# Forming the second 256 features' share of four heads' values one round earlier, beside the modulation

## The chip, the cores and the metric

The kernel runs on one core of one Trainium2 chip. The core has a matrix engine (TensorE, "PE" in the rows, with its weight loads as "PEld"), a vector engine (VectorE, "DVE"), a scalar engine (ScalarE, "ACT"), GpSimd ("POOL") and SyncE ("SP"), which here does nothing but issue transfers. Matrix results go to PSUM, which this kernel uses as eight banks of 128x512 float32. The metric is the time of one execution on the device, in microseconds (us); lower is better.

## The reference

One layer of a diffusion backbone: 256 latent tokens `x` and 256 context tokens `ctx`, each with 2048 features. What matters here is its beginning:

```python
mod = jax.nn.silu(c) @ w_mod[l] + b_mod[l]          # six vectors of 2048
sh_m, sc_m, ga_m, sh_f, sc_f, ga_f = split(mod)
hc = modulate(rms_norm(ctx, g), shc_m, scc_m)       # context, from silu(c_ctx)
h  = modulate(rms_norm(x, g), sh_m, sc_m)           # modulate(h, shift, scale) = h*(1+scale) + shift
p_i, p_ff, p_fb, p_q, p_g, p_cv, p_cg, p_gc, p_gh = split_proj(h @ w_in[l])
# context: only the first three parts of hc @ w_in
o = hgrn_bidir(q_prep(p_q), to_heads(p_i), hgrn_forget(p_ff), hgrn_forget(p_fb), ...)
```

So before any projection can be formed, the shift and the scale of a feature must be known, for the latent and for the context tokens. `p_i` are the values of 8 heads of 128 columns, for both kinds of tokens. A gated recurrence over the heads, a convolution branch, a gated merge, an output projection and a squared-ReLU MLP follow.

## The kernel before, in words

Every matrix product is formed in three terms: both factors are split into a high part and the rest (`hi`, `lo`), and hi*hi, hi*lo and lo*hi are added up in PSUM. A weight tile is 128x1024 float32 (512 KB). SyncE loads it into one of five `raw` buffers, ScalarE writes its `whi` (L123), VectorE its `wlo` (L126); each of these has four buffers. The class `Stream` holds the order of all loads as a list, `fetch_to` keeps up to 13 loads ahead, and a load into `raw` waits until the buffer's last reader is through. The order of the instructions on each engine is fixed when the program is built.

The front of the kernel computes the shift and the scale and uses them as soon as they are there. It is a loop over eight rounds `c = 0..7`, one for each 256 features. A round loads two `wmd` tiles (last 512 rows of the modulation weights, transposed), six `wm` tiles (its first 1536 rows, into `rawpage`), one `wi0` tile (256 rows of the input projection, columns of the first four heads' values) and in rounds 0, 1, 3 and 5 one `wf0` tile (forget gates of head 0). In a round

- VectorE forms eight sums of products with the `wmd` tiles (L648, four a tile),
- TensorE multiplies the `wm` tiles (`bank<-rawpage,s`, the modulation matmuls; the trace counts them as 24), ScalarE copies the sum (L605), TensorE turns it, VectorE makes scale and shift of it (L612 to L619),
- ScalarE and VectorE form the modulated features `h` (L629, L632), and VectorE multiplies the next round's inputs `xT` with their norm (L555),
- TensorE forms the values of the first four heads for these features (`values(0, ...)`, 24 matmuls a round in a steady order, half a round late) and the forget gates of head 0 (12 matmuls a round, `forget`).

The modulation matmuls stand at the end of a round's work: round c's other matmuls, then the modulation matmuls of round c + 1. In the rows below a round is counted from the end of its modulation matmuls.

The four accumulators of `values(0)` and the two of `forget` keep six of the eight banks through the front. One more product is formed there: the values of the *second* four heads over the *first* 256 features, from the tile `wi0[8]`, at the end of round 0 (`values_begun`): 24 matmuls, in two pairs of banks for the two kinds of tokens, copied to the pages `v1` by ScalarE. After the front, `values(1, ...)` forms the second four heads' values over the other seven tiles (`wi0[9]` to `wi0[15]`), and adds `v1` on VectorE at the end (L1322). This stretch is called the tail here. In it VectorE also begins the dot products of the other modulation vectors (L1244, tiles `wmt`), which need a row of silu(c) (`silu_row`, loaded at L1254 behind the front). The blocks of q and the heads follow.

`self.queued = []` ahead of the front makes TensorE keep the program's order there.

Of the kernel before, what the change touches and what calls it, by code (L numbers as in the profile page):

```python
# [8 lines left out]
F32 = mybir.dt.float32  # L9
# [4 lines left out]
ALU = mybir.AluOpType  # L14
# [4 lines left out]
KT = D // P  # L19
# [17 lines left out]
RAWS = 5  # L37
KP = 12
FETCH = 13

# [96 lines left out]
class Kernel:  # L137
# [227 lines left out]
    def run(self):  # L365
        nc, a = self.nc, self.a
# [3 lines left out]
        v = self.v  # L370
# [46 lines left out]
        for c in range(8):  # L417
            for u in range(2):
                st.add_whole(a["wmd"][2 * c + u])
            for t in range(KP // 2):  # L420
                st.add_whole(a["wm0"][KP // 2 * c + t], paged=True)
            st.add(a["wi0"][c])
            if c == 0 or c % 2 and c < 7:
                st.add(a["wf0"][(c + 1) // 2])
            if c == 0:
                st.add(a["wi0"][8])
        gq = collections.deque()
# [8 lines left out]
        def gemv(n):  # L436
            for _ in range(n):
                if gq:
                    st.add_gemv(*gq.popleft())
# [4 lines left out]

        for j in range(9, 16):
            st.add(a["wi0"][j])
            gemv(2)
        for b in range(16, 24):
# [215 lines left out]
        for c in range(8):  # L664
# [35 lines left out]
            if c % 2 and c < 7:  # L700
                parts(fq, *self.last2)
            if c < 7:
                normed(c + 1, *self.last2)
            for _ in range(2 if c else 1):
                next(values)
            for _ in range(2):
                next(forget)
            if c == 0:
                vb = self.values_begun(hx, vq2.popleft())
        for _ in values:  # L710
# [580 lines left out]
    def values(self, ch, hx, tiles, begun=None):  # L1291
# [3 lines left out]
        accs = [self.bank() for _ in range(4)]  # L1295
        for kq in range(begun is not None, 8):
            hi, lo = tiles()
            for k2 in range(2):
                k = 2 * kq + k2
                s = slice(k2 * 512, (k2 + 1) * 512)  # L1300
                cuts = [(accs[2 * i + tb], slice(tb * P, (tb + 1) * P), *hx(i)(k)[:2]) for i in range(2) for tb in range(2)]
                first, last = k == 2 * (begun is not None), k == KT - 1

# [22 lines left out]

    def values_begun(self, hx, w):

        nc = self.nc
        pages = self.pages(2, F32, "v1")  # L1330
        for i in range(2):
            accs = [self.bank() for _ in range(2)]
            for k in range(2):
                s = slice(k * 512, (k + 1) * 512)
                xh, xl = hx(i)(k)[:2]
                for tb in range(2):
# [4 lines left out]
            for tb in range(2):  # L1341
                self.last4 = nc.scalar.copy(out=pages[i][:, tb * 512:(tb + 1) * 512], in_=accs[tb])
        return pages
# [275 lines left out]
```

## Time and profile before

| | |
|---|---|
| median of 3 runs | 1643.31 us (1642.83 to 1644.01) |
| the profiled execution's own time | 1643.43 us |
| its span, first to last instruction | 1641.7 us |
| TensorE, matmuls busy | 1627.7 us (99%) |
| TensorE, weight loads busy | 1357.7 us (83%) |
| VectorE / ScalarE busy | 1163.2 us (71%) / 799.7 us (49%) |
| read from HBM | 370.93 MB |

A matmul counts as busy from its start to a modelled end; matmuls overlap, so a busy share of 99% means that there is nearly always one under way, not that none could be added. The 1.7 us between the span and the execution's time lie around the instructions. Times in rows count from the first instruction.

### The profile page before, as it was taken

The numbers are of one execution on the slowest core, as the hardware profiler recorded it, in microseconds if no ns is written. First come the engines' busy times: TensorE is split into PE (matmuls) and PEld (weight loads), VectorE is DVE, ScalarE is ACT, GpSimd is POOL, SyncE is SP. The second block draws the span as 40 slices with busy tenths as digits, with TensorE's granted clock in tenths as the row PEclk, the third lists the DMA queues.
The fourth block names the chain that finished last, engine by engine and source line by source line (L and its number), as shares of the span: only waits on it lengthen the run. The fifth ranks groups of instructions, "written<-read, shape, count | busy, mean of one in ns | idle before, by whom it ended". The sixth has DMA issues, their size and how long they took to land.

```text
span 1641.7 us, 22004 instructions
## 1 busy us (share of the span) xinstructions
PE 1627.7 (99%) x8207; PEld 1357.7 (83%) x8207; DVE 1163.2 (71%) x1702; ACT 799.7 (49%) x1141; POOL 8.1 (0%) x18
## 2 busy tenths in 40 slices
PE   8999999999999999999999999999999999999998
PEld 6668888888988888888788888888888888888887
DVE  7777877777868889967887766456655665566555
ACT  6553444343554444653446665445544554346543
POOL 0000000000000000000000000000000000000000
PEclk9999999999999999999999999999999999999999
DMA  9998954444656566678887466677666666665553
GB/s 378 392 395 293 316 166 141 154 142 142 207 189 224 187 192 206 230 271 306 313 289 260 143 230 205 214 235 241 218 206 231 234 213 217 230 219 195 190 193 116
DMA packets 103484, 374.47 MB, mean 228 GB/s; under 512 B 11601, under 2 KB 11857, under 8 KB 103377
## 3 DMA queue, kind: packets, MB, share of 16 engines
q1 hardware_dynamic: 101952, 368.60, 65.8%
q0 software_dynamic: 1280, 4.21, 0.8%
q8 instruction: 64, 1.05, 0.3%
q14 instruction: 44, 0.35, 0.1%
q10 hardware_dynamic: 144, 0.26, 0.0%
HBM read 370.93 MB, written 2.10 MB: 227 GB/s over the span
## 4 chain that ended last, share of the span: by engine, by line
PE 94%; DVE 2%; DMA 2%; ACT 1%; issue 1%; SPq 0%; DVEq 0%; ACTq 0%
PE bank L185 62%; PE bank L252 18%; PE bank L254 9%; PE bank L1391 2%; DMA x<-ctx 1%; DVE wlo L126 1%; DMA rawpage<-wm 1%; PE bank L1422 0%; DMA raw<-wpw 0%; PE bank L1433 0%; PE bank L1431 0%; ACT whi L123 0%; ACT h L629 0%; SPq L498 0%; ACT xT L629 0%
## 5 line engine op out<-in xcount | busy, mean ns | idle before, releaser
L126 DVE TENSOR_TENSOR wlo<-raw,whi 128x1024 fp32r<-128x1024 f32 x488 | 594.0, 1223 | 356.2 <-ACT whi L123 348.0
L123 ACT ACTIVATE whi<-raw 128x1024 fp32r<-128x1024 f32 x488 | 513.5, 1059 | 576.9 <-PE bank L185 320.7
L185 PE MATMUL bank<-whi,h 128*128 128x512 f32 x1264 | 396.3, 391 | 0.8 <-ACT h L629 0.5
L252 PE MATMUL bank<-h,whi 128*128 128x512 f32 x1280 | 322.3, 394 | 0.0
L185 PEld LDWEIGHTS bank<-whi,h 128*128 128x128 f32 x1264 | 237.1, 188 | 51.0 <-DVE h L1080 0.7
L252 PEld LDWEIGHTS bank<-h,whi 128*128 128x128 f32 x1280 | 230.4, 189 | 41.6
L185 PE MATMUL bank<-wlo,h 128*128 128x512 f32 x632 | 246.5, 390 | 0.8 <-DVE wlo L126 0.8
L185 PE MATMUL bank<-whi,hidh 128*128 128x512 f32 x503 | 195.1, 388 | 0.0
L185 PE MATMUL bank<-wlo,hidh 128*128 128x512 f32 x503 | 195.1, 388 | 0.0
L185 PE MATMUL bank<-whi,hidl 128*128 128x512 f32 x503 | 195.0, 388 | 0.0
L254 PEld LDWEIGHTS bank<-h,wlo 128*128 128x128 f32 x1280 | 174.6, 190 | 12.6
L254 PE MATMUL bank<-h,wlo 128*128 128x256 f32 x1280 | 178.4, 282 | 0.0
L185 PE MATMUL bank<-h,whi 128*128 128x512 f32 x512 | 164.6, 402 | 0.0
L185 PEld LDWEIGHTS bank<-wlo,h 128*128 128x128 f32 x632 | 118.7, 188 | 26.6 <-DVE wlo L126 2.5
L185 PEld LDWEIGHTS bank<-whi,hidl 128*128 128x128 f32 x503 | 94.4, 188 | 19.5
L185 PEld LDWEIGHTS bank<-wlo,hidh 128*128 128x128 f32 x503 | 94.5, 188 | 19.3
L185 PEld LDWEIGHTS bank<-whi,hidh 128*128 128x128 f32 x503 | 94.5, 188 | 19.2
L185 PEld LDWEIGHTS bank<-h,whi 128*128 128x128 f32 x512 | 92.0, 189 | 21.5 <-issue 5.9
L185 PE MATMUL bank<-h,wlo 128*128 128x512 f32 x256 | 100.0, 391 | 0.0
L1244 DVE SCALAR_TENSOR_TENSOR raw<-raw,silu_row 128x1024 f32<-128x1024 f32 x64 | 76.6, 1218 | 0.2 <-DMA raw<-wmt 0.2
L1231 DVE SCALAR_TENSOR_TENSOR gacc<-raw,silu_c,gacc 128x1024 f32<-128x1024 f32 x60 | 76.6, 1277 | 0.0
L185 PEld LDWEIGHTS bank<-h,wlo 128*128 128x128 f32 x256 | 48.1, 188 | 10.6 <-DVE wlo L126 0.3
(246 smaller groups left out, 1359.8 us busy)
## 6 DMA issues: line engine op xcount, KB each, us to landing
raw<-w SPq DMA_DIRECT2D x256, 512.0 KB, 4.2
raw<-wi SPq DMA_DIRECT2D x172, 512.0 KB, 4.4
raw<-wmt SPq DMA_DIRECT2D x64, 512.0 KB, 4.2
raw<-wm SPq DMA_DIRECT2D x64, 512.0 KB, 4.5
rawpage<-wm SPq DMA_DIRECT2D x48, 512.0 KB, 8.6
raw<-wo SPq DMA_DIRECT2D x32, 512.0 KB, 4.8
raw<-wmd SPq DMA_DIRECT2D x16, 512.0 KB, 8.2
raw<-who SPq DMA_DIRECT2D x16, 512.0 KB, 4.9
```

Source lines behind the costliest of these rows:

```text
L123: kn.his.append(nc.scalar.activation(out=hi, in_=raw, func=AF.Copy))
L126: kn.los.append(nc.vector.tensor_tensor(lo, raw, hi.bitcast(F32), op=ALU.subtract))
L185: ins = fn(*args, **kw)
L252: nc.tensor.matmul(bank, w[0][:, cut(i)], x(k)[2], start=(k == 0), stop=False)
L254: nc.tensor.matmul(bank[:, T:], w[1][:, cut(i)], x(k)[0], start=False, stop=(k == nk - 1))
L1231: nc.vector.scalar_tensor_tensor(acc, raw, s, acc, op0=ALU.mult, op1=ALU.add)
L1244: nc.vector.scalar_tensor_tensor(raw, raw, 1.0, self.srow, op0=ALU.mult, op1=ALU.mult, accum_out=self.dot[:, 32 * j + b:32 * j + b + 1])
L1391: nc.tensor.matmul(ps[:, b * P:(b + 1) * P], w, r, start=True, stop=True)
```

## The change

A constant `BEGUN = 2` says how many tiles of the second four heads' values are formed in the front. The tile `wi0[9]` is loaded at the end of round 1's loads and split there; `values_begun` runs in rounds 0 and 1, and the second time adds its result to the pages `v1` on VectorE, in place of ScalarE's copy. `values(1)` begins with `wi0[10]`. The loads of `wmt` that stood behind `wi0[9]` are given to the next tiles.

```diff
@@ Kernel.run, the list of loads
             st.add(a["wi0"][c])
             if c == 0 or c % 2 and c < 7:
                 st.add(a["wf0"][(c + 1) // 2])
-            if c == 0:
-                st.add(a["wi0"][8])
+            if c < BEGUN:
+                st.add(a["wi0"][8 + c])
...
-        for j in range(9, 16):
+        for j in range(8 + BEGUN, 16):
             st.add(a["wi0"][j])
-            gemv(2)
+            gemv(2 + (j < 12))
@@ the front's loop
             if c % 2 and c < 7:
                 parts(fq, *self.last2)
+            if c and c < BEGUN:
+                parts(vq2, *self.last2)
             if c < 7:
                 normed(c + 1, *self.last2)
...
-            if c == 0:
-                vb = self.values_begun(hx, vq2.popleft())
+            if c < BEGUN:
+                vb = self.values_begun(hx, vq2.popleft(), c, c and vb)
@@ values
-        for kq in range(begun is not None, 8):
+        begins = BEGUN * (begun is not None)
+        for kq in range(begins, 8):
...
-                first, last = k == 2 * (begun is not None), k == KT - 1
+                first, last = k == 2 * begins, k == KT - 1
@@ values_begun
-    def values_begun(self, hx, w):
+    def values_begun(self, hx, w, c, pages):
...
-        pages = self.pages(2, F32, "v1")
+        pages = pages or self.pages(2, F32, "v1")
...
-                xh, xl = hx(i)(k)[:2]
+                xh, xl = hx(i)(2 * c + k)[:2]
...
-                self.last4 = nc.scalar.copy(out=pages[i][:, tb * 512:(tb + 1) * 512], in_=accs[tb])
+                v = pages[i][:, tb * 512:(tb + 1) * 512]
+                if c:
+                    nc.vector.tensor_tensor(v, accs[tb], v, op=ALU.add)
+                else:
+                    nc.scalar.copy(out=v, in_=accs[tb])
```

On TensorE, at the end of round 1 (`h2` and `h3` are the features of round 1, `whi_400` the forget tile), before:

```order
L185 MATMUL bank_431<-h2_545,wlo_401 128x512
L185 MATMUL bank_432<-h2_545,whi_400 128x512 x2
L185 MATMUL bank_432<-h2_545,wlo_401 128x512
L185 MATMUL bank_615<-rawpage_488,s32_82 32x512 [waits DMAHW0_49,PE_49]
L185 MATMUL bank_615<-rawpage_488,s32_82 32x512
```

The forget gates are followed by the modulation matmuls of round 2. With the change (`whi_561`, `wlo_562` are of the tile `wi0[9]`; names in brackets are semaphores that the instruction waits for):

```order
L186 MATMUL bank_432<-h2_545,wlo_401 128x512
L186 MATMUL bank_596<-whi_561,h2_545 128x512 [waits Activation_49]
L186 MATMUL bank_596<-wlo_562,h2_545 128x512 [waits DVE_49]
L186 MATMUL bank_596<-whi_561,h2_545 128x512
L186 MATMUL bank_597<-whi_561,h2_545 128x512 [waits PE_49]
...
L186 MATMUL bank_612<-whi_561,h2_545 128x512 [waits DVE_49]
L186 MATMUL bank_612<-wlo_562,h2_545 128x512
L186 MATMUL bank_612<-whi_561,h2_545 128x512
L186 MATMUL bank_613<-whi_561,h2_545 128x512 [waits DVE_49]
...
L186 MATMUL bank_653<-rawpage_499,s32_82 32x512 [waits DMAHW1_49,DVE_49]
```

Between them stand 24 matmuls of the new tile, in the bank pairs 596, 597 (latent tokens) and 612, 613 (context tokens); the first of each of the second pair waits for VectorE, and so does the first modulation matmul of round 2.

On VectorE, from round 1's `xT` to round 2's `cols`, before (`junk` and `raw` are the eight sums for round 2):

```order
L555 TENSOR_TENSOR xT_110<-xT_110,s_82 128x1024
L126 TENSOR_TENSOR wlo<-raw,whi 128x1024
L648 SCALAR_TENSOR_TENSOR junk,part<-raw,srow 128x512 x2
L648 SCALAR_TENSOR_TENSOR raw,part<-raw,srow 128x512 x2
L648 SCALAR_TENSOR_TENSOR junk,part<-raw,srow 128x512 x2
L648 SCALAR_TENSOR_TENSOR raw,part<-raw,srow 128x512 x2
L653 TENSOR_TENSOR part<-part,pack 128x4
L612 TENSOR_REDUCE cols<-bank 128x8
```

and with the change:

```order
L556 TENSOR_TENSOR xT_110<-xT_110,s_82 128x1024
L127 TENSOR_TENSOR wlo<-raw,whi 128x1024 x2
L649 SCALAR_TENSOR_TENSOR junk,part<-raw,srow 128x512 x2
L649 SCALAR_TENSOR_TENSOR raw,part<-raw,srow 128x512 x2
L1348 TENSOR_TENSOR v_439<-bank,v_439 128x512 x2
L649 SCALAR_TENSOR_TENSOR junk,part<-raw,srow 128x512 x2
L649 SCALAR_TENSOR_TENSOR raw,part<-raw,srow 128x512
L1348 TENSOR_TENSOR v_440<-bank,v_440 128x512 x2
L649 SCALAR_TENSOR_TENSOR raw,part<-raw,srow 128x512
L654 TENSOR_TENSOR part<-part,pack 128x4 x2
L613 TENSOR_REDUCE cols<-bank 128x8
```

A second `wlo` stands ahead of the sums, and the four adds to `v1` stand among them.

On SyncE one load of `wi` is added behind round 1's `wf`, and the one of `wi0[9]` behind the front is gone; the order of the others is unchanged but for the `wmt` loads.

## Rows read from the trace of the kernel before

**Rows 1.** The page: its span, the busy times of the engines, and the clock that was granted to TensorE in 40 equal slices of the span (9 is 90% or more).

```profile
span 1641.7 us, 22004 instructions
PE 1627.7 (99%) x8207; PEld 1357.7 (83%) x8207; DVE 1163.2 (71%) x1702; ACT 799.7 (49%) x1141; POOL 8.1 (0%) x18
PEclk9999999999999999999999999999999999999999
```

**Rows 2.** Busy times in windows: rounds 1 to 6 of the front, each from the end of its modulation matmuls to the end of the next round's, and the tail; between them lies round 7 with the end of the front. Columns: the window and its length, busy us of each engine (and instructions), granted clock, share of the DMA engines, GB/s.

```profile
43.63:55.20 11.57, 11.57 (x69) 7.67 (x65) 7.79 (x18) 6.54 (x11) 0.00 (x0) 1.00 1.01 395
55.20:66.79 11.59, 11.59 (x68) 7.67 (x65) 9.30 (x28) 5.60 (x10) 0.00 (x0) 1.00 1.02 410
66.79:80.08 13.29, 12.84 (x68) 7.71 (x64) 11.01 (x30) 6.55 (x11) 0.00 (x0) 1.00 0.97 370
80.08:92.05 11.97, 11.97 (x66) 7.79 (x65) 9.69 (x29) 5.59 (x10) 0.00 (x0) 1.00 1.02 409
92.05:104.67 12.62, 12.62 (x66) 7.79 (x64) 9.89 (x26) 6.54 (x11) 0.00 (x0) 1.00 1.03 409
104.67:116.22 11.55, 11.55 (x66) 7.73 (x64) 9.26 (x27) 5.60 (x10) 0.00 (x0) 1.00 1.03 409
129.07:167.15 38.08, 38.08 (x169) 31.53 (x168) 30.83 (x45) 11.35 (x13) 0.00 (x0) 1.00 0.86 307
```

**Rows 3.** The list of waits of TensorE's weight loads in rounds 1 to 7 (43.6 to 130): who waited for whom, us in total, times, the longest.

```profile
PEld bank L185 <- DMA rawpage<-wm: 4.4, 7, 1.1
```

**Rows 4.** The chain of work that ended last, in round 3 (60 to 82): start, length, what; and SyncE's own time line for the pairs of `wmd` loads of rounds 4 and 6 (start of the first issue, time to the end of the second).

```profile
65.41 1.23 DVE raw L648 x4
66.66 0.33 SPq L85
...
70.02 9.04 DMA rawpage<-wm
79.10 3.10 PE bank L185 x14
...
59.41 7.58 SPq L85 DMA_DIRECT2D raw<-wmd  x2
84.20 6.75 SPq L85 DMA_DIRECT2D raw<-wmd  x2
```

**Rows 5.** TensorE's time line at the end of round 1: the last forget matmuls and the modulation matmuls of round 2.

```profile
52.17 0.39 PE L185 MATMUL bank<-h,wlo 128*128 128x512 f32 x1
52.48 2.78 PE L185 MATMUL bank<-rawpage,s 128*32 128x512 f32 x24
```

**Rows 6.** VectorE's time line in rounds 1 and 2 (the first three rows of round 1, the last two are the first and the fourth sum for round 3), and ScalarE's in round 1.

```profile
50.41 1.22 DVE L555 TENSOR_TENSOR xT<-xT,s 128x1024 f32<-128x1024 f32 x1
51.54 1.22 DVE L126 TENSOR_TENSOR wlo<-raw,whi 128x1024 fp32r<-128x1024 f32 x1
52.68 0.69 DVE L648 SCALAR_TENSOR_TENSOR junk<-raw,srow 128x512 f32<-128x512 f32 x1
64.10 0.68 DVE L648 SCALAR_TENSOR_TENSOR junk<-raw,srow 128x512 f32<-128x512 f32 x1
65.94 0.68 DVE L648 SCALAR_TENSOR_TENSOR raw<-raw,srow 128x512 f32<-128x512 f32 x1
...
49.67 1.04 ACT L123 ACTIVATE whi<-raw 128x1024 fp32r<-128x1024 f32 x1
55.34 0.59 ACT L605 COPY row<-bank 128x512 f32<-128x512 f32 x1 [4.62 <-PE bank L185]
```

**Rows 7.** The add of a bank to `v1` on VectorE, at the end of the tail: shortest, median and longest ns.

```profile
L1322 DVE TENSOR_TENSOR v<-bank,v x4: 686/690/691, 165.3 to 168.4; 128x512 f32<-128x512 f32 x4
```

**Rows 8.** The loads of line L85 from 5 to 135 us: time from issue to landing.

```profile
DMA to landing us min/median/max: 3.1/9.0/10.9
```

**Rows 9.** The end of the front and the tail in the time lines of SyncE (the load of the tail's third tile, the load of the row of silu(c), the load of the tail's fourth tile), VectorE (third `wlo`, first and second dot product, fourth and fifth `wlo`) and ScalarE (third `whi`, the gates, the row's sigmoid, fourth `whi`).

```profile
125.12 0.33 SPq L85 DMA_DIRECT2D raw<-wi  x1
125.98 0.42 SPq L1254 DMA_DIRECT2D silu_row<-crow  x1
136.28 0.33 SPq L85 DMA_DIRECT2D raw<-wi  x1
...
129.63 1.23 DVE L126 TENSOR_TENSOR wlo<-raw,whi 128x1024 fp32r<-128x1024 f32 x1 [4.53 <-ACT whi L123]
133.87 1.23 DVE L1244 SCALAR_TENSOR_TENSOR raw<-raw,silu_row 128x1024 f32<-128x1024 f32 x1
135.03 1.22 DVE L1244 SCALAR_TENSOR_TENSOR raw<-raw,silu_row 128x1024 f32<-128x1024 f32 x1
142.01 1.23 DVE L126 TENSOR_TENSOR wlo<-raw,whi 128x1024 fp32r<-128x1024 f32 x1 [1.18 <-ACT whi L123]
146.74 1.23 DVE L126 TENSOR_TENSOR wlo<-raw,whi 128x1024 fp32r<-128x1024 f32 x1 [1.12 <-ACT whi L123]
...
128.53 1.06 ACT L123 ACTIVATE whi<-raw 128x1024 fp32r<-128x1024 f32 x1
130.91 1.09 ACT L598 ACTIVATE fg<-bank 128x512 f32<-128x512 f32 x2
131.88 1.15 ACT L1263 ACTIVATE sig<-silu_row 128x512 f32<-128x512 f32 x2
140.92 1.06 ACT L123 ACTIVATE whi<-raw 128x1024 fp32r<-128x1024 f32 x1 [7.89 <-DMA raw<-wi]
```

More of the change, by code (lines that the diff above doesn't have):

```diff
@@ L38 @@
 KP = 12
+BEGUN = 2
 FETCH = 13
```

## The prediction

> **What bounds the kernel now.** I read the page first. TensorE (PE) is busy 99% of the span at full granted clock [rows 1], so nothing far from PE can give much, and work that is only moved pays exactly where PE waits today. The windows, cut at the end of each round's modulation matmuls, show where that is: the rounds last 11.57, 11.59, 13.29, 11.97, 12.62 and 11.55 us [rows 2]. A round holds the same PE work each time, so 11.57 is PE's own need, and what lies above it (1.72 + 0.40 + 1.05, less 0.02 = 3.15 us) is waiting. The list of waits names whom: PE's weight loads for `rawpage<-wm`, 4.4 us in 7 waits [rows 3], a part of which lies beside running matmuls. The transfers move 409 GB/s at a share of 1.03 in an undisturbed round and only 370 at 0.97 in the round of 13.29 us [rows 2]: there the queue ran thin. The chain says why [rows 4]: VectorE (DVE) ended four sums at 66.64, this freed a `raw` buffer, SyncE issued at 66.66, and six loads later, at 79.06, PE went on. So the front has two bounds that lie close together, PE (11.57 a round) and the transfers, and the second hangs on DVE's sums through five buffers.
>
> **The change, part by part.**
>
> *Taken out and put in.* 24 matmuls leave the tail and enter the end of round 1, where in front of the 12 modulation matmuls PE had nothing between 52.17 and 52.48 [rows 5]. A tile of values is 24 matmuls; in the tail seven of them (168) take 38.08 us [rows 2], so one is 5.44 us, 0.2267 a matmul. Their price is the same in both places; this is no gain by itself.
>
> *Waits in round 1.* The new matmuls need the new tile's `wlo`. On DVE it stands behind `wlo` of the forget tile, which starts at 51.54 and is followed at 52.68 by the next instruction [rows 6]; so the new one runs 52.68 to 53.9 (1.22 each). PE can start its first new matmul at 52.40, the second only at 53.92: 1.3 us lost. All eight banks are in use then (4 values, 2 forget, 2 that alternate), so the two pairs of accumulators and the next modulation bank pass through two banks; each waits for an add on DVE. An add of this form takes 0.69 us [rows 7]. Pair 1 is complete with the ninth and the twelfth matmul, whose ends are 53.92 + 7 x 0.2267 + 0.39 = 55.9 and 56.6; DVE's first four sums last 2.52 us as in the next round (64.10 to 66.62) [rows 6], hence to 56.3, and the adds end at 57.0 and 57.6. Pair 2 starts at 57.0 instead of 56.4 (0.55 lost). Its adds stand behind three more sums (a quarter of 2.52 each), the first runs 59.4 to 60.1, and only then the modulation matmuls of round 2 start: 60.09 against 52.48. Sum: 5.44 + 1.3 + 0.55 + 0.3 = 7.6 us later. Round 2 begins at 62.8 instead of 55.20. ScalarE is no bound: the new tile's `whi` follows the one at 49.67, ahead of 4.6 us of idle time [rows 6].
>
> *What PE gets back.* With no wait at all PE would run 5 rounds of 11.57 from 62.8 and begin round 7 at 120.65; before it was 116.22 [rows 2]. So the front ends at least 4.4 us later: 7.6 less the 3.15 of waits.
>
> *What the loads do.* One load more in round 1 is 512 KB at 409 GB/s, 1.28 us. More important is the buffer ring. The second `wmd` load of round 4 takes the buffer of the first of round 3, so it waits for DVE's first four sums for round 3, which stand behind round 2's whole chain. In round 1 `xT` starts 6.78 us after the round's begin (43.63 to 50.41) and lasts 1.13, then 2.52 us of sums [rows 6]: with round 2 at 62.8 the load is issued at 73.3, not 66.66. Meanwhile the queue has little: the loads before it were issued long ago and are through at about 70 (69 plus the 1.28). Upper bound for the way from this issue to the last modulation load of round 4: what it takes now, 66.66 to 79.06, 12.4 us [rows 4]; lower bound: the shortest landing of this line, 3.1 us [rows 8], plus six transfers of 1.28, 10.8 us. This gives 84.1 to 85.7; I take 85.0, nearer the present case, since that one too restarted behind a thin queue. PE goes on 1.02 us after that landing (79.06 to 80.08), so round 4 begins at 86.0, just where PE alone would be (85.95). From there 28 transfers (nine a round and one forget tile) follow each other to the last modulation load of round 7: 28 x 1.28 = 35.8, so 120.8, and round 7 begins at 121.9. Delay at the front's end: 5.65 us, bounds 4.4 (PE alone) and 6.4 (85.7 instead of 85.0).
>
> The Trainium skill's page "DMA: Bandwidth & Descriptors", section "Anatomy of one DMA — SWDGE (gpsimd) path", gives a DMA a fixed 2.0 us plus its bytes at 436 GB/s, here an estimate of 3.2 us for the first load and 1.2 for each that follows: 83.7 instead of 85.0, and PE alone would then set the pace (the second rival). No row splits a transfer into these two parts; the shortest landing, 3.1 us [rows 8], lies near that estimate.
>
> *The tail.* Its values have 24 matmuls less: -5.44. But the third of its six tiles was not early. Before, its `wlo` ended at 143.24, and PE needed it at 129.07 + 3 x 5.44 + 0.23 = 145.62 [rows 2, 9]: 2.38 us ahead, as the fourth tile from the tail's begin. Now it is the third, needed 5.44 us sooner after the tail's begin. What it waits for is not PE: its load takes the buffer that the second dot product frees (136.25, issue 136.28), the dots wait for the row of silu(c), and that row's load is issued behind the last tile that the front's end prepares [rows 9]. All this starts from round 7 and moves with it. Only ScalarE has one `whi` less ahead of the gates, which may bring the row's sigmoid (131.88) up to 0.4 us forward, to the landing of its data. So PE waits 5.44 - 2.38 - 0.4 = 2.65 us in the tail. Tiles four to six are ready in time: the next had 147.97 against 151.06 (3.1 ahead) and keeps its distance to the third. The blocks behind have weights some microseconds ahead, and nothing later in the program is changed.
>
> **Sum**: +5.65 - 5.44 + 2.65 = +2.9 us. The profiled execution took 1643.43 us; with 2.9 that is 1646.3. The median of the runs is 1643.31, so the profile's own time stands 0.12 above it, less than the runs differ among themselves. 0.2% of it is 3.3 us, about what a measurement of this kernel can tell from no change; the chances below go by it.
>
> **The rivals.**
> 1. *The forecast*: loads pace the front, the tail gives back half. 1646.3, own range 1645.5 to 1647.0 (delay 4.9 to 6.4). Chance 0.35.
> 2. *PE alone paces the front*: the queue restarts at the lower bound or faster (3.1 us is among its landings). +4.4 - 5.44 + 2.65 = +1.65: 1645.1. The queue's full share right after short gaps speaks for it, the 13.29 us round against it. Chance 0.2.
> 3. *The tail gives all back*: the third tile of the tail is not late, because less of its chain hangs on round 7 than I read. +5.65 - 5.44 = +0.2: 1643.6. For it: ScalarE and DVE idle 7.9 and 4.5 us around the front's end [rows 9]. Against: the idle is waiting for these very loads. Chance 0.17.
> 4. *Faster*: the new matmuls fall wholly into PE's waits for loads, with no new ones. It ends at -3.15, 1640.3, and cannot end lower, since no PE work is removed. It decides from the point where less than 3 of the 7.6 us reach round 4's loads. Against it: the waits that are to be filled lie in rounds 3 to 6, the added work in round 1, and the loads are freed by DVE behind the same chain. Chance 0.08.
> 5. *The queue runs dry a second time*: in round 6 a `wmd` load waits for sums again (now issued by 90.95, a pair that takes 6.75 us to issue, after 7.58 for round 4 [rows 4]). By my count it is issued at 86.0 + 6.78 + 1.13 + 2.52 = 96.4 and lands from 99.5 on, while the twelve loads ahead of it are through at 100.4 and its own turn ends at 101.7: 2 us to spare. If these are used up, a restart like round 4's loses another 2 us and more: 1648.3 and up. Chance 0.2.
>
> **Numbers.** The range for 8 in 10 leaves out rival 4 and the upper half of 5: 1642.8 to 1648.4. Slower by over 0.2% (above 1646.6): two fifths of 1 (0.14), nearly all of 5 (0.19), and 0.05 for delays that I put too low in 2 and 3: 0.38. Faster by over 0.2% (below 1640.0) only from the end of rival 4: 0.05. Within: 0.57.
>
> **What would show it.** Right: 24 matmuls `whi,h`/`wlo,h` at 52.4, with waits of PE for DVE ahead of the second, the 13th and the next modulation matmuls; round 2 at 62.8; a gap of some 5 us in the transfers between 70 and 75; round 7 at about 121.9; a wait of PE for `wlo` of 2 to 3 us, 11 us into the tail; the tail's values done at about 170 (167.15 before). Wrong: rounds 2 to 6 that still show waits as long as now; a tail without a wait; a front that ends less than 4 us later.

## The result

| | before | with the change |
|---|---|---|
| median of 7 runs each | 1644.01 us (1642.83 to 1645.35) | 1649.75 us (1647.96 to 1651.29) |
| ratio, 95% interval | | 1.0033 (1.0024 to 1.0043) |
| the profiled execution, its span | 1643.43 us, 1641.7 us | 1650.39 us, 1648.6 us |

The change makes the kernel slower, by 5.4 us by the ratio (forecast: 2.9 slower, range up to 1648.4). Two later comparisons on other chips gave 1.0025 (1.0015 to 1.0034) and 1.0025 (1.0016 to 1.0034), +4.1 us. The sign was right, the size too small.

The page of the changed kernel, span and busy times, against [rows 1]:

```profile
span 1648.6 us, 22010 instructions
PE 1630.0 (99%) x8207; PEld 1357.5 (82%) x8207; DVE 1166.3 (71%) x1706; ACT 800.4 (49%) x1141; POOL 8.1 (0%) x18
```

The windows of the changed kernel, cut as in [rows 2]: rounds 1 to 6, the tail, and the first 3.76 us after its wait (columns as there: busy us of PE, PEld, DVE, ACT, POOL, granted clock, DMA share, GB/s):

```profile
43.99:63.21 19.22, 17.70 (x92) 12.02 (x88) 14.14 (x32) 7.50 (x12) 0.00 (x0) 1.00 0.98 376
63.21:74.80 11.59, 11.59 (x68) 7.67 (x65) 7.79 (x19) 5.60 (x10) 0.00 (x0) 1.00 0.64 247
74.80:86.71 11.91, 11.91 (x69) 7.79 (x65) 9.60 (x26) 6.54 (x11) 0.00 (x0) 1.00 0.97 370
86.71:99.48 12.77, 12.59 (x66) 7.74 (x64) 10.49 (x31) 5.60 (x10) 0.00 (x0) 1.00 1.03 408
99.48:112.28 12.80, 12.64 (x67) 7.76 (x65) 9.87 (x28) 6.55 (x11) 0.00 (x0) 1.00 1.03 410
112.28:123.94 11.66, 11.66 (x67) 7.72 (x65) 9.28 (x29) 5.60 (x10) 0.00 (x0) 1.00 1.03 408
136.76:173.78 37.02, 34.58 (x146) 27.91 (x144) 26.28 (x39) 10.05 (x12) 0.00 (x0) 0.95 0.80 290
150.24:154.00 3.76, 3.76 (x10) 2.77 (x11) 3.67 (x5) 0.02 (x1) 0.00 (x0) 0.58 1.01 402
```

Round 1 has grown from 11.57 to 19.22 us (+7.65). Rounds 2 to 6 were to give 1.92 back (59.1 between the forecast begins of rounds 2 and 7, 62.8 and 121.9; 3.15 was the bound with no wait left). They last 60.73 instead of 61.02: they gave 0.29. The tail, 24 matmuls shorter, lasts 37.02 instead of 38.08: it gave 1.06, where 5.44 less a wait of 2.65, or 2.79, was forecast. The last two rows tell why: PE is busy for only 34.58 of 37.02 us, and the clock granted right after the wait is 0.58. Between its two levels, 1.2 and 2.4 GHz, that is mostly the lower.

The sum is 7.65 - 0.29 - 1.06 = 6.3; 0.36 of the other 0.6 us stands ahead of round 1, which begins at 43.99 instead of 43.63. Such a shift comes without any change: in three profiles of the changed kernel round 1 begins at 43.34, 43.70 and 43.99, over all profiles below between 43.3 and 45.5. So the times that follow count from round 1's begin in the same profile.

Two lists of the changed kernel. First PE's time line at the end of round 1 (in brackets what it waited for), to be held against [rows 5]:

```profile
52.78 0.39 PE L186 MATMUL bank<-whi,h 128*128 128x512 f32 x1
54.32 0.50 PE L186 MATMUL bank<-wlo,h 128*128 128x512 f32 x1 [1.15 <-DVE wlo L127]
57.37 0.50 PE L186 MATMUL bank<-whi,h 128*128 128x512 f32 x1 [0.26 <-DVE v L1348]
60.50 2.78 PE L186 MATMUL bank<-rawpage,s 128*32 128x512 f32 x24
```

And the waits of PE's weight loads from 40 to 180, against [rows 3]:

```profile
PEld bank L186 <- DMA rawpage<-wm: 3.9, 6, 1.1
PEld bank L186 <- ACT whi L124: 2.9, 1, 2.9
PEld bank L186 <- DVE wlo L127: 2.0, 2, 1.6
PEld bank L186 <- DVE v L1348: 1.2, 2, 0.7
```

The old waits for `wm` loads are still there (3.9, before 4.4). Of the new kinds, `wlo` and `v` belong to round 1 but for 0.4 us, and the 2.9 us for `whi` to the tail.

### The profile page after: what moved, and what is told of

It is laid out like the page before. It is cut to its first block, busy times and chain, and to the rows that moved or that the text cites. A ratio compares the mean times of both kernels' runs of the same rounds, so it can differ in the third digit from the quotient of the medians.

```text
span 1648.6 us, 22010 instructions
## 1 busy us (share of the span) xinstructions
PE 1630.0 (99%) x8207; PEld 1357.5 (82%) x8207; DVE 1166.3 (71%) x1706; ACT 800.4 (49%) x1141; POOL 8.1 (0%) x18
## 4 chain that ended last, share of the span: by engine, by line
PE 89%; DMA 5%; DVE 3%; ACT 1%; issue 1%; SPq 0%; DVEq 0%; ACTq 0%
PE bank L186 58%; PE bank L253 18%; PE bank L255 9%; PE bank L1399 2%; DMA rawpage<-wm 1%; DVE wlo L127 1%; DMA raw<-wpw 1%; DMA raw<-wf 1%; DMA x<-ctx 1%; ACT whi L124 0%; PE bank L1430 0%; ACT h L630 0%; PE bank L1441 0%; PE bank L1439 0%; DMA silu_row<-crow 0%
## 5 line engine op out<-in xcount | busy, mean ns | idle before, releaser
L186 PEld LDWEIGHTS bank<-whi,hidh 128*128 128x128 f32 x503 | 94.5, 188 | 19.2
```

The source lines that it names most:

```text
L186: ins = fn(*args, **kw)
```

## The experiments

Of each profile four times are compared, all read from PE's time line: round 2's and round 7's begin and the end of the tail's values (start of the first matmul of the q block), counted from round 1's begin, and the rest, from there to the end of the span.

| kernel | round 2 | round 7 | values done | rest | ratio to before, 95% interval |
|---|---|---|---|---|---|
| before | 11.57 | 72.59 | 123.52 | 1474.55 | |
| forecast | 19.2 | 78.3 | 126.4 | as before | 1.0018 |
| changed | 19.22 | 79.95 | 129.79 | 1474.82 | 1.0033 (1.0024, 1.0043) |
| after_again | 19.23 | 80.05 | 127.77 | 1474.83 | 1.0025 (1.0015, 1.0034) |
| after_3 | 19.23 | 79.70 | 129.61 | 1474.95 | 1.0025 (1.0016, 1.0034) |
| a_tail | 19.24 | 80.26 | 125.77 | 1474.52 | 1.0006 (0.9997, 1.0015) |
| a_swap | 18.00 | 78.14 | 127.66 | 1474.66 | 1.0025 (1.0016, 1.0034) |
| a_st | 18.00 | 78.44 | 123.93 | 1474.47 | 1.0002 (0.9994, 1.0011) |
| a_mm | 17.60 | 77.68 | 127.66 | 1475.06 | 1.0023 (1.0013, 1.0033) |
| a_paged | 19.26 | 77.55 | 127.64 | 1474.60 | 1.0027 (1.0016, 1.0039) |
| a_all | 18.04 | 76.37 | 121.88 | 1475.40 | 0.9988 (0.9979, 0.9997) |
| a_best | 17.36 | 75.71 | 121.23 | 1474.51 | 0.9983 (0.9975, 0.9992) |
| b_paged | 11.60 | 71.41 | 122.37 | 1474.40 | 0.9989 (0.9980, 0.9998) |
| b_load | 12.58 | 74.46 | 125.39 | 1474.86 | 1.0008 (0.9999, 1.0017) |
| b_wait | 11.58 | 72.50 | 128.41 | 1474.85 | 1.0028 (1.0017, 1.0039) |
| b_wait2 | 11.59 | 72.99 | 129.11 | 1474.18 | 1.0021 (1.0012, 1.0030) |
| b_wfill | 11.58 | 72.77 | 126.69 | 1477.95 | 1.0020 (1.0011, 1.0029) |
| a_fill | 19.24 | 79.42 | 127.43 | 1474.84 | 1.0032 (1.0019, 1.0044) |
| a_fill2 | 19.23 | 79.69 | 128.37 | 1475.02 | 1.0027 (1.0017, 1.0038) |

### The tail: a wait, and the clock behind it

**after_again**, the changed kernel once more.

> The changed kernel once more, beside the others. What the profile showed so far: 1650.39 us against 1643.43, of which the front's end is 7.7 later (round 7 at 123.94 instead of 116.22), the tail 1.1 shorter. Theory 'wait and clock': the wait of 2.4 us ahead of the tail's third tile is followed by a stretch at half clock every time, so the clock over the first us after that wait is about 0.6, and the ratio to the kernel before is 1.0033 to 1.0042 (+5.5 to +7). Rival 'chance': the low clock was an accident of one execution; then this profile has a clock of 1.00 there and the kernel takes 1.8 us less, +3.7 to +5.

PE's time line at the third tile of its tail, and the windows over the time behind it:

```profile
149.22 1.21 PE L186 MATMUL bank<-whi,h 128*128 128x512 f32 x4 [1.56 <-ACT whi L124]
```

```profile
149.22:153.00 3.78, 3.73 (x15) 2.77 (x16) 3.50 (x5) 0.29 (x1) 0.00 (x0) 1.00 1.01 390
```

Here the wait was 1.56 us, the clock stayed at 1.00, and the last four tiles took 171.47 - 149.22 = 22.25 us; in the profile above it was 2.44 us and they took 173.78 - 150.24 = 23.54. So the fall does not come every time, and it came with the longer wait. As expected for 'chance', the clock was 1.00 here and the kernel took +4.1 us. Neither theory had said that the wait itself would vary.

**a_tail** loads the third tile ahead of four of the six `wmt` tiles that stood in front of it, all of which wait for the row of silu(c).

```diff
         for j in range(8 + BEGUN, 16):
             st.add(a["wi0"][j])
-            gemv(2 + (j < 12))
+            gemv(1 + 2 * (j > 11))
```

> The changed kernel, with the third tile of the tail loaded ahead of four of the dot products' tiles instead of behind six; all is computed. Theory 'wait and clock': the wait of 2.6 us is gone, and with it the 1.8 us that the tail loses at half clock: 4.4 less than the changed kernel, the tail's values take 24 matmuls x 6 x 0.2267 = 32.6 us, total +1.5 to +2.5 against the kernel before. Rival 'wait only' (the clock falls for another reason): 2.6 less, +3 to +4.4. Rival 'given back' (the dots come later and hold up the blocks behind): no less than now, +5.5 to +7.

Its tail in the windows:

```profile
136.99:169.68 32.69, 32.69 (x145) 27.04 (x145) 25.05 (x38) 9.14 (x11) 0.00 (x0) 1.00 0.83 304
```

No wait, clock 1.00, and 32.69 us: 144 matmuls at 0.227. The kernel is at 1.0006, some 3 us below after_again on the same chip; the rest of the program has not grown (1474.52). 'Given back' and 'wait only' are out: the tail's wait, with what came behind it, cost some 3 us of the 4.1.

**b_wait** makes the same kind of wait in the kernel before, where nothing else is changed but the order of the tail's loads.

```diff
         for j in range(9, 16):
             st.add(a["wi0"][j])
-            gemv(2)
+            gemv(6 if j == 11 else 1 + (j < 11))
```

> The kernel before, with six instead of two of the dot products' tiles loaded ahead of the tail's fourth tile (and fewer behind it); nothing of the front is touched and all is computed. Its load comes as late as that of the sixth transfer after the first dot product now, about 147, so PE must wait 2 to 3 us there. Theory 'wait and clock': the wait is followed by a stretch at half clock that costs 1.8 more: +4 to +5. Rival 'wait only': the granted clock stays 1.00, +2 to +3. Rival 'slack behind': the blocks take it up, 0 to +1.

PE waited 2.27 us, the clock behind it was 0.69 over 3.9 us, and the last four tiles took 172.95 - 148.63 = 24.32 us: +4.6 by the ratio, as the first theory said. That the clock fell because PE was idle, and not because of the transfers there, is for the second pair to tell: **b_wait2**, the same once more, and **b_wfill**, which puts idle work into the wait:

```diff
+            third = begun is not None and kq == 4
+            if third:
+                with self.tc.issue_after(mine.ins):
+                    mine = self.warm(18)
...
```

The rest of the edit puts the fourth tile's first matmuls in the changed kernel's order (four with `whi`, then four with `wlo`) and keeps the program's order there.

> The kernel before with six of the dot products' tiles loaded ahead of the tail's fourth tile, once more, as the partner of the next one on the same chip. It waited 2.27 us at that tile, after which the granted clock was 0.69 over 148.6 to 152.5 and the last four tiles took 24.3 us. Both theories: +4 to +5.5 against the kernel before, four tiles in 23.5 to 24.5.

> The same with 18 small matmuls on a constant (result not used; about 2.1 us) between the third and the fourth tile, in the wait, and the fourth tile's first matmuls in the changed kernel's order (four with the first part of the weights, then four with the second). Theory 'clock follows idleness': the fourth tile still begins where its load lets it, but the granted clock is 1.00 and the last four tiles take 22.3 us: 1.3 to 2 us less than its partner, +2.5 to +3.5. Rival 'clock falls anyway' (for instance because of the transfers that run there): the clock is about 0.65 after the small matmuls too, four tiles in 23.5 or more, as its partner.

PE's time line of b_wait2 at the fourth tile, and its windows behind it:

```profile
149.02 0.73 PE L185 MATMUL bank<-whi,h 128*128 128x512 f32 x2 [2.49 <-ACT whi L123]
```

```profile
150.00:152.00 2.00, 1.72 (x4) 1.43 (x5) 1.76 (x4) 1.06 (x1) 0.00 (x0) 0.59 1.04 408
152.00:154.00 2.00, 2.00 (x6) 1.51 (x6) 1.98 (x3) 0.95 (x1) 0.00 (x0) 0.55 0.72 256
```

The same of b_wfill:

```profile
145.60 2.12 PE L185 MATMUL bank<-ones_r 128*128 128x128 f32 x18
148.09 1.19 PE L185 MATMUL bank<-whi,h 128*128 128x512 f32 x4 [0.37 <-ACT whi L123]
```

```profile
150.00:152.00 2.00, 2.00 (x11) 1.61 (x10) 1.76 (x4) 0.64 (x1) 0.00 (x0) 1.00 1.01 360
152.00:154.00 2.00, 2.00 (x10) 1.69 (x9) 1.76 (x3) 1.06 (x1) 0.00 (x0) 1.00 0.69 215
```

The tile begins at the same distance from round 7 (31.8 and 31.7 us), the transfers run alike (1.04 and 1.01, 0.72 and 0.69), and beside the order of the fourth tile's first eight matmuls only PE's idleness differs: the clock is 0.59 and 0.55 in the one, 1.00 in the other, the four tiles take 24.30 and 22.26 us. So the half clock follows from the idleness, not from the transfers; the changed kernel, which has that order too, fell with a wait and not with a filled one (below). On the median, though, b_wfill is only 0.6 us below its partner (1648.48 and 1649.05), not 1.3 to 2, and its profile shows where the profiled execution gave the gain back. PE's time line in a later stretch, b_wfill and then b_wait2:

```profile
801.99 0.50 PE L185 MATMUL bank<-wlo,h 128*128 128x512 f32 x1 [1.64 <-DVE wlo L126]
```

```profile
802.76 0.50 PE L185 MATMUL bank<-wlo,h 128*128 128x512 f32 x1 [0.25 <-DVE wlo L126]
```

There PE waits for VectorE; arriving earlier it waited longer, and the clock fell once more (the rest is 1477.95 instead of 1474.18). This is not what every execution does. The mean granted clock over the span is known for each, and the profiles with one such fall read 0.998: so do ten of b_wait2's eleven executions, but of b_wfill's eleven only the profiled one. So the small matmuls keep the clock nearly always, and yet the median gains only 0.6 us; where the others lose the rest of the gain is not shown.

**a_fill** and **a_fill2** (with **after_3** as its partner) fill the wait of the changed kernel with 14 and 18 small matmuls.

> The changed kernel, with 14 small matmuls on a constant (their result is not used; some 1.8 us) between the tail's second and third tile, where PE waits; nothing else differs. Theory 'clock follows idleness': the third tile begins where it did (its load decides), some 26 us after round 7, but the granted clock stays 1.00 and the tail's last four tiles take 22.2 us, as in the one execution whose clock did not fall, instead of 23.5: 1.3 less than the changed kernel, +2.3 to +4. Rival 'clock falls anyway' (something else than PE's idleness lowers it): 23.5 for the four tiles, +4 to +6.

> The changed kernel a third time, as the partner of the next one. Both theories: the wait at the tail's third tile is 1.6 to 2.6 us, and the four tiles take 23.5 us when the clock falls behind it, 22.3 when not; +4 to +6.

> The changed kernel with 18 small matmuls on a constant in the tail's wait (result not used). Theory 'clock follows idleness': four tiles in 22.3 us in every profile, and on the median 0.7 to 1.5 less than its partner, since the partner's clock falls in some executions only. Rival: the same as its partner.

PE's time line of a_fill at the third tile, then of after_3:

```profile
146.78 1.68 PE L186 MATMUL bank<-ones_r 128*128 128x128 f32 x14
148.72 1.20 PE L186 MATMUL bank<-whi,h 128*128 128x512 f32 x4 [0.26 <-ACT whi L124]
```

```profile
149.34 1.50 PE L186 MATMUL bank<-whi,h 128*128 128x512 f32 x4 [2.41 <-ACT whi L124]
```

after_3 waited 2.41 us, its clock fell, and its four tiles took 23.61; in a_fill and a_fill2 the clock stayed at 1.00 and they took 22.34 and 22.31. But the medians do not show it: 1649.17 for a_fill2 against 1649.58, and a_fill at 1.0032 is no better than the changed kernel. The mechanism is shown by the profiles. How often it strikes, the mean clocks tell: of the changed kernel's 27 executions (7, 9 and 11) 13 read 0.998, with a median of 1650.55 us, and 14 read 0.999 or 1.000, with 1648.76. That is 1.8 us between them, in which longer waits may have a part, in about half of the executions; over all of them the fall makes some 0.9 of the 4.1 to 5.4 us.

### The front: loads, buffers, sums

**a_swap** splits the new tile ahead of the forget tile of round 1.

```diff
+            if c and c < BEGUN:
+                parts(vq2, *self.last2)
             if c % 2 and c < 7:
                 parts(fq, *self.last2)
-            if c and c < BEGUN:
-                parts(vq2, *self.last2)
```

(and the two loads in the same order)

> The changed kernel, with the new tile loaded and split ahead of the forget tile of round 1, which is used only in round 3; all is computed. The 1.15 us that PE waits for the new tile's second half goes. Theory 'chain' (round 4's loads hang on VectorE's sums, these on the begin of round 2): round 2 begins at 62.1 instead of 63.2, the second load of the pair for round 4 is issued 1.1 earlier (72.6), and round 7 begins 1.1 earlier, at 122.8: 1.1 less in all, +4.5 to +6 against the kernel before. Rival 'transfers': the number of transfers alone paces the rounds 4 to 7, round 7 stays at 123.9 and nothing is gained.

Round 2 begins 1.23 us earlier than in after_again, the `wmd` load behind the sums is issued at 28.5 after round 1 instead of 29.7, and round 7 begins 1.9 earlier. 'Chain' holds: where round 2 begins decides where the loads of round 4 begin. Yet the kernel is not faster (1.0025 both). PE's wait in the tail, and the windows behind it:

```profile
149.01 1.60 PE L186 MATMUL bank<-whi,h 128*128 128x512 f32 x4 [2.10 <-ACT whi L124]
```

```profile
149.00:152.50 3.50, 3.49 (x9) 2.60 (x10) 3.50 (x5) 0.08 (x1) 0.00 (x0) 0.59 1.02 410
```

From round 1's begin, round 7 came 1.9 us earlier than in after_again and the tail's third tile only 1.4 (104.13 and 105.52), so the wait grew and the clock fell. **a_st** (a_swap and a_tail together) asks whether that is the reason.

> The changed kernel with two repairs: the new tile split ahead of the forget tile, and the third tile of the tail loaded ahead of four of the dot products' tiles; all is computed. Theory 'the tail is a gate' (its third tile decided when the tail ended, so what the swap gained in the front was lost there): now it is seen, round 7 begins 78.1 after round 1, no wait in the tail, 1.8 less than with the tail repaired alone (+1.0): -0.8 against the kernel before. Rival 'not a gate': the swap brings nothing here either, +1.0.

Without the tail's wait the swap is seen: its values are done 1.84 us before a_tail's, as much as the front gained. The time went from 1.0006 to 1.0002, 0.7 us of the 1.8 expected; the intervals overlap.

**a_mm** has the new matmuls without the new load.

```diff
-            if c < BEGUN:
-                st.add(a["wi0"][8 + c])
+            if c == 0:
+                st.add(a["wi0"][8])
...
+            if c == 1:
+                vq2.append(vq[-1])
...
-            if c and c < BEGUN:
-                parts(vq2, *self.last2)
```

> The changed kernel without the load and the split of the new tile: the 24 new matmuls of round 1 take the weights of the first four heads for these features, which are split already, so the second four heads' values lack their right share of the second 256 features; the rest is computed as in the change. Theory 'chain' (the load is hidden, as assumed): round 2 begins 17.9 after round 1, and round 7 78.1 after it, as with the two splits swapped. Rival 'the load counts too' (alone, without matmuls, it made round 7 come 1.9 later): round 7 76.9 after round 1 or less. The total says little, since the tail's wait stays: +2 to +5.

Round 2 and round 7 both begin 0.4 to 0.5 us earlier than in a_swap, which has the load: beside the delayed round 2 the load costs nothing. 'Chain' holds again. The counterpart is **b_load**, the load without the matmuls.

```diff
-            if c == 0:
-                st.add(a["wi0"][8])
+            if c < 2:
+                st.add(a["wi0"][8 + c])
...
+            if c == 1:
+                parts(vq2, *self.last2)
```

> The kernel before, with one load more in round 1: the tile wi0[9] is loaded and split there as in the change, but not used; the tail loads it again as before, and all is computed. Theory 'chain': without the new matmuls round 2 begins where it does now and the transfers have the room (the queue runs dry in rounds 2 and 3 as it is), so round 7 begins at most 0.6 later: 0 to +0.6. Rival 'one transfer more': the front is paced by its transfers and round 7 begins 1.3 later or more: +1.3 to +2.5.

Its round 1 in the windows, and its waits of PE for `wm` loads (6.3 us, before 4.4):

```profile
43.65:56.23 12.58, 12.58 (x69) 7.79 (x65) 8.79 (x17) 7.50 (x12) 0.00 (x0) 1.00 0.97 374
```

```profile
PEld bank L185 <- DMA rawpage<-wm: 6.3, 8, 1.1
```

My expectation was wrong: alone, the load makes round 1 1.0 us longer and round 7 1.87 later. The kernel before has not 1.3 us of room in its transfers; in the change the load is free only because the matmuls are late by more.

**a_paged** and **b_paged** take the `wmd` tiles out of the ring of five buffers.

```diff
-FETCH = 13
+FETCH = 15
...
-                st.add_whole(a["wmd"][2 * c + u])
+                st.add_whole(a["wmd"][2 * c + u], paged=True)
...
-            if out.count(False) > RAWS or out.count(True) > FETCH - RAWS:
+            if out.count(False) > RAWS or out.count(True) > 10:
```

> The changed kernel, with the wmd tiles of the front loaded into pages (10 of them allowed ahead, together with the wm tiles) instead of the five raw buffers; all is computed. Theory 'ring': only because a wmd load waits for VectorE's sums does the queue run dry at 70 to 74; without that PE alone paces the rounds, 11.6 each from round 2 on, the transfers show no gap there, and round 7 begins 58.0 us after round 2 instead of 60.8: 2.8 less than the changed kernel, with its tail's wait still there, +1 to +3.5 against the kernel before. Rival 'transfers': the queue has as many loads as it can move anyhow; rounds 4 to 6 stay above 12, nothing is gained, +4 to +5.5.

> The kernel before, with the wmd tiles loaded into pages in the same way; all is computed. Theory 'ring': the waits of PE for the loads of rounds 4 and 6 go as far as the transfers allow: 43 loads of 1.28 after the one that landed at 58.4 give 113.5 for round 7's last one, 1.7 earlier than now; so -1.7 (-3.1 if PE alone paces). Rival 'transfers' (the queue is full as it is): 0.

The transfers from 70 to 74, in the changed kernel and in a_paged (queue, packets, MB, share of 16 engines):

```profile
q1 hardware_dynamic: 40, 0.13, 7.9%
```

```profile
q1 hardware_dynamic: 452, 1.64, 103.1%
```

And a_paged's rounds 1 to 6 in the windows:

```profile
45.06:64.32 19.26, 17.71 (x93) 12.03 (x89) 14.14 (x32) 7.50 (x12) 0.00 (x0) 1.00 1.03 409
64.32:75.92 11.60, 11.60 (x69) 7.67 (x65) 7.79 (x19) 5.60 (x10) 0.00 (x0) 1.00 1.03 407
75.92:87.52 11.60, 11.60 (x69) 7.67 (x65) 9.28 (x26) 6.55 (x11) 0.00 (x0) 1.00 0.99 387
87.52:99.13 11.61, 11.61 (x69) 7.67 (x65) 9.33 (x29) 5.60 (x10) 0.00 (x0) 1.00 1.01 394
99.13:110.73 11.60, 11.60 (x69) 7.67 (x65) 9.31 (x24) 6.55 (x11) 0.00 (x0) 1.00 0.99 385
110.73:122.61 11.88, 11.88 (x69) 7.51 (x65) 9.59 (x29) 5.60 (x10) 0.00 (x0) 1.00 0.96 377
```

Without the ring the queue has no gap, and in the changed kernel PE alone paces the rounds. That the edit also lets 15 loads run ahead instead of 13 is not separated from it. In the changed kernel it gives 2.4 us in the front, and again the tail takes them: its wait was 2.60 us and the clock fell. In the kernel before it gives 1.2 us at round 7, which stay to the end of the values (122.37 instead of 123.52), and 1.8 by the ratio (0.9989); there two rounds still last 12.39 and 12.72 us.

**a_all** puts the three repairs together; **a_best** moreover completes one half of the tokens first, so that the adds come earlier (this part is shown).

```diff
-            for k in range(2):
-                s = slice(k * 512, (k + 1) * 512)
-                xh, xl = hx(i)(2 * c + k)[:2]
-                for tb in range(2):
+            for tb in range(2):
+                for k in range(2):
+                    s = slice(k * 512, (k + 1) * 512)
+                    xh, xl = hx(i)(2 * c + k)[:2]
```

> The changed kernel with three repairs at once: the new tile split ahead of the forget tile in round 1, the third tile of the tail loaded ahead of four of the dot products' tiles, the wmd tiles in pages; all is computed. If the three losses are what the single runs say and they add: 5.3 of 5.4 us for the new matmuls come back in the tail, round 2 begins 6.0 later, the waits of 3.1 in rounds 3 to 6 are filled, no wait in the tail and a clock of 1.00: -2 us against the kernel before, down to -2.6. Rival 'another bound': something that the three hide today (the transfers of rounds 4 to 7, VectorE's sums) comes up, and it stays within 0.5 us of a_tail or above the kernel before: 0 to +1.

> The three repairs together, and the new matmuls (and those of round 0) taken in another order, first all of one half of the tokens, so that each bank is complete, and added on VectorE, six matmuls earlier; all is computed. Theory 'banks': the waits of PE for the adds (0.55 and 0.3) go, round 2 begins 17.2 after round 1 instead of 18.0, and the total is 0.8 below that of the three repairs: -2.8 against the kernel before. Rival 'VectorE' (the adds stand ahead of the sums for round 2, which come later, and PE waits for what follows them): no gain, -2 or worse.

The windows of a_best, round 1, round 2 and the tail:

```profile
43.76:61.12 17.36, 17.36 (x92) 12.09 (x88) 13.43 (x29) 7.49 (x12) 0.00 (x0) 1.00 1.03 409
61.12:72.75 11.63, 11.63 (x68) 7.67 (x64) 8.54 (x25) 5.59 (x10) 0.00 (x0) 1.00 1.03 408
132.25:164.99 32.74, 32.74 (x146) 27.09 (x145) 24.87 (x38) 9.31 (x11) 0.00 (x0) 1.00 0.84 305
```

Both came out as summed from the single runs: -2.0 and -2.8 us. PE has no gap left in these stretches; a_best beats both kernels. But a_all is level with b_paged, on the same chip and without the move (0.9988 and 0.9989): a repaired ring alone is worth as much. What a_best's order of the matmuls, which changes those of round 0 too, would give the kernel before was not run.

## Why the prediction was wrong in size

The path was the right one: waits in round 1, loads that hang on VectorE's sums, a tail that waits for its third tile. Two terms of the sum were too small: the delay at the front's end, said 5.65 and measured 7.36 us, and what the tail loses, said 2.65 and measured 37.02 - 144 x 0.2267 = 4.38.

- *Waits in round 1*: right, to 0.05 us. 53.92, 57.0, 60.09 and 62.8 were said; with the 0.36 of this execution's later begin, 54.32, 57.37, 60.50 and 63.21 were read. The price 0.2267 a matmul and the adds of 0.69 held.
- *The load behind the sums*: said 73.3, read 73.69; the queue nearly empty from 70 to 74 (share 7.9%) as said. Round 4 was put at 86.0 (86.4 with the shift) and came at 86.71: from that issue to the last modulation load of round 4 it took 12.0 us (12.4 and 12.3 in the two other profiles), forecast 11.7 between bounds of 10.8 and 12.4. The value taken was too low, the upper bound nearly right. The estimate that the prediction made from the Trainium skill's page "DMA: Bandwidth & Descriptors", section "Anatomy of one DMA — SWDGE (gpsimd) path", 3.2 + 6 x 1.2 = 10.4 us, was lower still. The section's figures are for DMAs on GpSimd's path, these loads are issued by SyncE, and the measured 12.0 decides. In three profiles of the changed kernel round 4 begins 42.7 to 43.2 after round 1, forecast 42.4.
- *The step that failed in the front* is "28 transfers follow each other, 28 x 1.28 = 35.8". From round 4 to round 7 it took 37.23, 36.87 and 36.65 us in the three profiles. The same stretch in the profile of before, 80.08 to 116.22 [rows 2], is 36.14: reading it whole, and not multiplying one transfer's time, would have shown part of it. Nearly all the excess lies in round 4 (12.77, where nine transfers are 11.5), with the queue full. With the later restart this makes the delay at round 7 7.36 us and not 5.65.
- *What PE gets back*: 1.92 of the 3.15 was in the forecast, 0.29 came. Rival 2 is out, and so is 4; with the wait in the tail rival 3 is out too.
- *Tail, the wait*: said 2.65, read 2.60 from the end of the second tile (147.64) to the third (150.24). That the two agree is in part luck. Said was a wait for `wlo`, with the chain from round 7 up to 0.4 us earlier. Read was a wait for `whi`, which ended 26.25 after round 7's begin and before 25.76, so the chain was 0.5 later; in the program's new order four matmuls with `whi` stand ahead of the first with `wlo`, and behind them PE waited some 0.5 us more (four tiles in 22.25 us in after_again, with the clock at 1.00, where 4 x 5.44 is 21.76). That the wait hangs on the tile's load, and so on the second dot product, agrees with ScalarE's time line:

```profile
149.13 1.06 ACT L124 ACTIVATE whi<-raw 128x1024 fp32r<-128x1024 f32 x1 [7.72 <-DMA raw<-wi]
```

- *Tail, the clock*: the second step that failed, by omission. "So PE waits 5.44 - 2.38 - 0.4 = 2.65 us in the tail" prices the wait at its own length. In the profiles where PE was idle there for 2.10 to 2.87 us (seven of them) the granted clock fell to 0.5 to 0.7, and the last four tiles took 23.2 to 23.6 us in the changed kernel's order instead of 22.3: 1.3 us more. After 1.56 us, and wherever the wait was filled, it stayed at 1.00 there. The Trainium skill, "TensorE: Matmul & The Clock Gate", section "HAM oscillation — how this bites in real kernels", describes matmuls that are slow after a wait for transfers because the clock has fallen meanwhile; these traces agree, with 0.58 behind the wait, and it was not drawn on in the prediction.
- *Rival 5* (the queue runs dry a second time): did not happen, the share in rounds 4 to 6 is 1.03. Its price, 1648.3 and up, was near the result for another reason.

Together, on the profiled execution: 1646.3 + 1.7 (front) + 1.7 (tail: clock 1.3 and the second wait 0.5, -1.06 instead of -2.79) + 0.36 (before round 1) + 0.3 (rest) = 1650.4, and 1650.39 was measured.

What stays open is why round 4 takes 0.8 to 1.3 us more than its nine transfers in the three profiles of the changed kernel. One landing has it all. In the profile above the load issued at 84.37 landed after 6.4 us and the next one, issued at 84.89, after 8.6:

```profile
84.37 0.42 SPq L86 DMA_DIRECT2D rawpage<-wm  x1
rawpage<-wm SPq DMA_DIRECT2D x1, 512.0 KB, 6.4
84.89 0.38 SPq L86 DMA_DIRECT2D rawpage<-wm  x1
rawpage<-wm SPq DMA_DIRECT2D x1, 512.0 KB, 8.6
```

That is 90.8 and 93.5, 2.7 us apart, where the other loads of rounds 4 to 6 land 1.12 to 1.40 apart. Between them two transfers of program code fall into the full queue; the transfers from 90 to 94.5:

```profile
q8 instruction: 1, 0.02, 1.5%
q14 instruction: 1, 0.01, 0.5%
```

1.5% and 0.5% of 16 engines over 4.5 us are 1.1 and 0.4 us of one engine. If that engine falls behind by as much and every load needs all engines, all landings behind are late by 1.4 us until the queue runs empty. The Trainium skill has both halves: in "Runtime: NRT & Kernel Launch", section "Instruction fetch mechanics", the engines' code comes in blocks of 16 KiB by a DMA queue of its own, with which the q8 row agrees, while the q14 row has half as much; and in "DMA: Bandwidth & Descriptors", section "Why a DMA increments its semaphore by 16 and not by 1", a transfer counts as landed only when each engine has reported, which no run here isolates. The two other profiles of the changed kernel and the one of before have one landing 0.9, 0.8 and 0.5 us late behind the like block. In b_wait it strikes one load later, 0.4 us, so that round 4 lasts 11.56 us there and round 5 pays, with 13.20 for ten loads of 1.28:

```profile
92.28:105.48 13.20, 12.88 (x69) 7.80 (x65) 10.86 (x30) 6.58 (x11) 0.00 (x0) 1.00 1.03 410
```

But in b_paged both kinds fall into a full queue at 89 to 91, and the loads land 1.24 to 1.29 us apart all the same. So this is argued, not shown.

## What to carry to other kernels

Work moved from a stretch without waits into one with waits gains at most those waits, and only if what paces them is not itself moved: here the loads hung on sums that stood behind the moved work, so the waits moved along. Price a new wait of PE by its length and by what runs at half clock behind it, and look at what was next in line before: a tile that was 2.4 us early is a wait when 5.4 us of cover go. Where a queue runs dry because of a buffer ring, free the ring first; here that gave as much alone as with the move.

## What had not been expected of the hardware

- The granted clock fell after idle stretches of PE of 2.10, 2.27, 2.41, 2.44, 2.49, 2.60 and 2.87 us in the tail, to means of 0.5 to 0.7 over the next 3.5 to 4 us, and after 1.64 us in b_wfill at 802, where 0.51 us had gone before at 797; not after 1.56 us in the tail, nor after 1.15 to 1.18 us in round 1. Eighteen matmuls of 128 columns (2.12 us) in such a gap kept it at 1.00.
- A stretch of the front with a full queue (share 1.02 to 1.03, 404 to 408 GB/s) delivered nine loads in 12.77 us in one profile and in 11.56 in another: the share of the queue does not say when the loads land.
- The begin of round 1 varied by 2.2 us between profiles of kernels that are alike up to there.
